# Two stored operands fewer, and the chopped-up sums of the fourth product on another timetable, in a soft-routing MoE kernel

## The chip, the cores and the metric

The kernel runs on one core of one Trainium2 chip. The metric is the device time of one execution in microseconds; the median of the runs counts, lower is better.

## The reference

Every token goes through all eight experts, and the results are added with the softmax of its router logits as weights:

```python
probs = softmax(router_logits)                       # 16 x 512 x 8
for e in range(8):
    output += probs[:, :, e:e+1] * (x @ expert_weights[e])
# x: 16 x 512 x 512, expert_weights: 8 x 512 x 2048, output: 16 x 512 x 2048, float32
```

## The kernel before

**One large product.** The sum over the experts is one matrix product `Z W`. `Z` has 8192 rows (tokens) and 4096 columns (the product of a probability and `x`, for each expert and each of 512 inputs). `W` holds the eight expert matrices one below the other. Operands are f16, sums f32.

**Seven products in place of eight, twice.** `Z` is cut into 16 row pairs `q`; each has a block `a = 2q` and a block `b = 2q + 1` of 256 rows. Its columns are cut into experts 0 to 3 and 4 to 7, and `W` into two halves of columns. A Strassen-like scheme makes the result of a row pair from seven products, P1 to P7, of sums of these quarters. Each is cut again in the same way into seven steps, in the order `STEPS = (1, 5, 6, 2, 7, 3, 4)`. A step is eight matmuls of 128x128 by 512 columns into one PSUM bank. The steps of the inner scheme use three banks of a product in turn: bank `x` for the steps 1, 6, 7 and 4, bank `q` for 5 and 3, bank `b` for 2. After a step, VectorE (DVE) or ScalarE (ACT) reads the bank (`post`), so a bank must have been read before the next step that uses it.

**Left operands** (class `Left`) are made on DVE from `x` (tile `xT`), probabilities that a DMA spreads over the partitions (`pT`) and a scratch tile `u`. For P5 it is `x_b` times the sums of the probabilities of both halves (`PQ`). P6 takes this one less `x_a` times `P1`. P7 takes `x_a P1 - x_b P1` (two products and a difference for each half). P3 wants `x_a P2` less the operand of P6, so every operand of P6 is stored in DRAM (`keep_z`, two transfers of 512 KB, tensor `z`) and fetched again as one of 1 MB (`ZBlock`).

**Right operands** are made from the weights by DVE and kept in 15 tiles `w` of 1 MB (pool `wpool`). Two products run side by side, which takes 14 of them. The sums for P7 and P4 don't fit beside them. `by_parts` makes them in the 15th tile, in four *quarters* each. A quarter goes through three hooks: `begin` loads four pieces (POOL's queue), `go_on` (P4 alone) subtracts `t2` from three of them and stores the differences as `t4` (`less_t2`), and `end` makes four sums in place (`sums_in_place`), each overwriting a piece and each stored at once (`wd<-w`, POOL's queue). Before the products begin, `turnover` fetches the 1 MB operands one by one through ACT's queue (`fetch_w`, line 164, `w<-wd`).

**Stages and slots.** `add` lists 56 stages, numbered from 0, of one or two products. In a stage with two, the steps alternate, 14 slots of 8 matmuls each. Stage 15 is `k5`: P5 of the pairs 0 and 1. Stage 16 is P6 of pair 0 alone. Stages 17 to 30 pair P6 of `q` with P5 of `q + 1`. Stage 31 (`k7`) is P6 of pair 15 and P7 of pair 0, stages 32 to 46 pair P4 of `q` with P7 of `q + 1`. Stage 47 (`k3`) is P4 of pair 15 and the first P3, stages 48 to 54 hold two P3 each, and stage 55 (`end`) the P3 of pair 15, which writes the result out itself. "21:8" below is slot 8 of stage 21. Counting matmuls along the trace puts the start of stage 17 at 437.0 us, of 21 at 533.7, of 22 at 557.9, of 23 at 584.1, of 28 at 710.8, of 31 at 784.0, of 32 at 811.2, of 46 at 1151.6, of 47 at 1175.8 and of 54 at 1340.2.

**Order.** The order of all instructions is written out by hand, and each engine works through its own in order. `at(stage, slot, make)` hooks a piece of work to a slot; `slots_after` counts slots on from a place. DVE's work goes into a `queue` of tasks with costs: `slack` lets out as many after each slot as a planned clock has room for, and `later(..., True)` puts a task ahead of the queue. `joined` (three tasks at the slots 12 and 13, a fourth at slot 3) is such: it takes P5's result from a tile of stored sums `h<-kept`, fetched by SP's queue. `start_loads` issues the loads of the stage after next after the first slot (`late` and `wait_for` change that slot, and the slot from which the left operands are queued).

Of the kernel before, what the change touches and what calls it, by code (L numbers as in the profile page):

```python
# [31 lines left out]
def kernel(  # L32
# [87 lines left out]
    def pool(o, i, **how):  # L120
        note(nc.gpsimd.dma_start(out=o, in_=i, **how))  # L121
# [12 lines left out]
    def new_w():  # L134
        return wpool.tile([P, K8, NB], f16, name="w", tag="w")
# [66 lines left out]
    P1, P2, PQ = 0, HE, 2 * HE  # L202
# [167 lines left out]
    def flush(task):  # L370
        while task is not None and not task.done:
            queue.popleft().run()

    def need(task):
        if task is not None and not task.done:
            flush(task)
            clock["pe"] = max(clock["pe"], clock["dve"])
# [244 lines left out]


    QK = 9
    ND = QK // 2

    def out_rows(q, odd, cols, tn):
        t, n = tn
        return out_f[ds((2 * q + odd) * HQ + t * HP, HP), ds(cols * NH + n * NB, NB)]

    def to_out(q, odd, cols, **how):
        return lambda tn, o: pool(out_rows(q, odd, cols, tn), o, **how)
# [18 lines left out]
    hooks, late, wait_for = {}, {}, {}  # L651

    def at(stage, slot, make):
        hooks.setdefault((stage, slot), []).append(make)

    def add(*products):
        stages.append(products)
        return len(stages) - 1
# [6 lines left out]
    def xblock(h):  # L665
        if h not in xs:
            xs[h] = XBlock(h)
        return xs[h]

    def left_of(r, q, fresh=True):  # L670
        a, b = 2 * q, 2 * q + 1
        if r == 1:
            pt = PBlock(a, P1, xp1[q - 2][1] if q in (2, 3) else None)
            if q in (2, 3):
                xs[a] = XBlock(a, xp1[q - 2][0])
            return Left(xblock(a), pt), [xblock(a), pt]
        if r in (2, 4):
            h, pt = (a, PBlock(a, P2)) if r == 2 else (b, PBlock(b, P2))
            return Left(xblock(h), pt), [xblock(h), pt]
        if r == 5:  # L680
            pt = PBlock(b, PQ)
            return Left(xblock(b), pt), [xblock(b), pt]
        if r == 6:
            pt = PBlock(a, P1)
            return Left(xblock(a), pt, of=lefts[5, q]), [xblock(a), pt]
        if r == 3:
            pt, kept_z = PBlock(a, P2), ZBlock(q)
            return Left(xblock(a), pt, kept=kept_z), [xblock(a), pt, kept_z]
        pa, pb = PBlock(a, P1), PBlock(b, P1)
        return Left(xblock(a), pa, (xblock(b), pb)), [xblock(a), pa, xblock(b), pb]  # L690

    def kept_rows(q):
        return lambda tn: kept[q][tn[1], ds(tn[0] * HP, HP), :]

    def product(r, q, **how):
        left, loads = left_of(r, q)
        lefts[r, q] = left
        p = None
        if r == 1:
            def sink(tn, o):  # L700
                pool(kept_rows(q)(tn), o)
            p = Product(right[1], left, sink)
        elif r == 2:
            if q >= QK:
                base = products[1, q].o.__getitem__
            else:
                base = bases[2, q] = Base(kept_rows(q))
            p = Product(right[2], left, to_out(q, 0, 0), base)
        elif r == 5:
            bases[6, q] = m1 = Base(kept_rows(q))  # L710
            m1.task = {}

            p = Product(right[5], left, to_out(q, 1, 0))
        elif r == 6:
            m1 = bases[6, q]

            def base(tn):
                need(m1.task[tn])
                return m1.t[tn]
            p = Product(right[6], left, to_out(q, 0, 1), base)  # L720
        elif r == 7:
            base = bases[7, q] = Base(lambda tn: out_rows(q, 0, 1, tn))
            p = Product(right[7], left, to_out(q, 1, 1), base)
        elif r == 4:
            p = Product(right[4], left, to_out(q, 1, 0, accum_op=ADD), products[7, q].o.__getitem__)
        else:
            p = Product(right[3], left, to_out(q, 0, 1, accum_op=ADD), **how)
        p.loads = loads
        products[r, q] = p
        return p  # L730
# [121 lines left out]

    for q in range(2, QK, 2):
        add(product(1, q), product(1, q + 1))
    for q in range(QK, 15):
        add(product(2, q), product(1, q + 1))
    forget(*range(0, 2 * QK, 2))
    rest = [15] + list(range(QK))
    for i in range(0, QK + 1, 2):
        k = add(product(2, rest[i]), product(2, rest[i + 1]))  # L860
# [5 lines left out]
    k5 = add(product(5, 0), product(5, 1))  # L866
# [3 lines left out]
    some = product(6, 15)  # L870
# [3 lines left out]
        add(product(4, q), product(7, q + 1))  # L874
    some = product(4, 15)
    xs.clear()
    k3 = add(some, product(3, 0))
    for q in range(1, 15, 2):
        add(product(3, q), product(3, q + 1))
    end = add(product(3, 15))  # L880
    late[k3 - 1] = 6
# [11 lines left out]
    for q in range(16):  # L893
        k = k5 + 1 + q
# [37 lines left out]
    def wedge_at(stage, slot, kn, e, then):  # L932
        made = []

        def begin():
            casts, made_ = wedge(kn, e)
            casts()
            made.extend(made_)

        def go_on():  # L940
            for make in made:
                later(1.22, make)
        at(stage, slot, begin)
        at(*then, go_on)

    b21, t1, t2, t3 = {}, {}, {}, {}
# [7 lines left out]
    def sums_at(stage, slot, r, of, ps):  # L954
        def go():
            if right[r].w is None:
                right[r].sums = right[r].build(of)
            for p in ps:
                right[r].queue_sum(right[r].sums, p)
        at(stage, slot, go)  # L960
    sums_at(ND - 1, 3, 2, b21, (5,))
    sums_at(ND - 1, 5, 2, b21, (6,))
    sums_at(ND - 1, 7, 2, b21, (7,))
    sums_at(ND - 1, 12, 2, b21, (4,))
    for i, (kn, e) in enumerate((kn, e) for kn in ((0, 0), (1, 0), (1, 1)) for e in range(2)):
        wedge_at(ND + i, 2, kn, e, (ND + i, 11))

# [60 lines left out]
    def slots_after(stage, slot, n):  # L1028
        slot += n
        while slot >= 7 * len(stages[stage]):  # L1030
            slot -= 7 * len(stages[stage])
            stage += 1
        return stage, slot
# [6 lines left out]
    def by_parts(stage, slot, every, r, load, between, when):  # L1040

        for j in range(4):
            b, chunks = {}, ds(2 * j, 2)

            def begin(b=b, j=j, chunks=chunks):
                flush(last_part[0])
                t = new_w()
                for i, kn in enumerate(ORDER):
                    b[kn] = t[:, ds(2 * i, 2), :]
                    load(b[kn], kn, j, chunks)  # L1050

            def go_on(b=b, chunks=chunks):
                for kn in b:
                    if kn != ODD:
                        between(b[kn], kn, chunks)

            def end(b=b, chunks=chunks):
                last_part[0] = sums_in_place(lambda p, o: pool(part_of((r, p), (0, 0), chunks), o), b, r, 0.69)
            at(*slots_after(stage, slot, j * every), begin)
            if between is not None:  # L1060
                at(*slots_after(stage, slot, j * every + when[0]), go_on)
            at(*slots_after(stage, slot, j * every + when[-1]), end)
# [8 lines left out]
    def load_part(what):  # L1071
        def load(t, kn, j, chunks):
            pool(t, part_of(what, kn, chunks))
        return load
# [10 lines left out]
    def keep_raw(t, kn, chunks):  # L1085
        pool(part_of("b22", kn, chunks), t)

    by_parts(k5 + 2, 4, 14, 7, load_part("t3"), None, (7,))
    by_parts(*slots_after(k5 + 2, 4, 60), 24, 4, load_p4, less_t2, (8, 15))
    by_parts(k7 + 4, 4, 36, 3, cast_part(22), keep_raw, (9, 16))  # L1090


# [16 lines left out]
    turnover(k7, 0, 4, "t4")  # L1109
    turnover(k3 - 1, 1, 3, "b22", 2)  # L1110

    for q in range(16):
        z_dram[q] = dram.tile([P, 2 * K8, HQ], f16, name=f"z_{q}")

        def keep_z(k, q=q):
            sp(z_dram[q][:, ds(k * K8, K8), :], lefts[6, q].t[k])
        k, half_way = k5 + 1 + q, 7 * len(stages[k5 + q]) * 9 // 14
        at(k - 1, half_way, lambda keep_z=keep_z: keep_z(0))
        at(k, 0, lambda keep_z=keep_z: keep_z(1))

    def load_z(q):
        load = products[3, q].loads[-1]
        load.by_hook = True
        return load.begin
    at(k3, 0, load_z(1))
    at(k3, 2, load_z(2))
    third3 = {}

    def third_of_p3(p):
# [2 lines left out]
        later(2.76, make)  # L1132
    at(k3, 3, lambda: third_of_p3(1))
    at(k3, 5, lambda: third_of_p3(5))
    wait_for[k3] = 7


    finish = products[3, 15]
# [33 lines left out]

    for stage in range(1, ND):
        thirds[stage] = Thirds(*(p.left for p in stages[stage]), third)
# [44 lines left out]
```

## Time and profile before

| | us |
|---|---|
| runs: median (lowest, highest) of 3 | 1383.44 (1380.64, 1385.46) |
| the profiled execution: its own time | 1381.43 |
| its span, first to last instruction | 1379.7 |
| TensorE matmul (PE) busy | 1362.8 (99%) |
| VectorE (DVE) busy | 1121.1 (81%) |
| GpSimd (POOL) busy | 411.6 (30%) |
| ScalarE (ACT) busy | 206.8 (15%) |

The profile is of one execution. Its span is 1.7 us shorter than the time of that execution, and that time is 2.0 us below the median of the runs. PE is TensorE's matmuls, PEld its weight loads, SPq and ACTq the queues through which SyncE and ScalarE issue DMAs. In rows of groups, `out<-in` names the tiles; behind the bar stand busy time, mean duration in ns, and the idle time of the engine just before, with what ended it. In rows of waits the three numbers are the sum, the count and the longest. In rows of windows each engine has its busy time and, in brackets, its instructions; then come the granted share of TensorE's clock, the share of the DMA engines and GB/s.

### The profile page before, as it was taken

Reading aid. Unit: us, or ns where it says so; the run is one execution under the profiler, and the core shown is the slowest. Engines: PE = TensorE matmul, PEld = TensorE weight load, DVE = VectorE, ACT = ScalarE, POOL = GpSimd, SP = SyncE. Lnnn points to the kernel's source line nnn. Section 1 sums busy time; section 2 is a strip of 40 time slices with the busy share of each in tenths; the row PEclk is TensorE's granted clock in tenths of the full one; section 3 lists DMA queues with packets and bytes.
Section 4 is the critical chain, followed back from the end, with each engine's and each line's share of the span. In section 5 each row is a group of like instructions: output and inputs, shape, how many; then the busy total and the mean of one; then the engine's idle time right before and its main releaser. Section 6 shows DMA issues by size and latency. Waiting matters only on the chain.

```text
span 1379.7 us, 18165 instructions
## 1 busy us (share of the span) xinstructions
PE 1362.8 (99%) x6630; PEld 645.9 (47%) x6630; DVE 1121.1 (81%) x1354; ACT 206.8 (15%) x397; POOL 411.6 (30%) x652
## 2 busy tenths in 40 slices
PE   9999999999999999989999989999999999999998
PEld 4555444444444444434444434444444444556554
DVE  7877767579789898588878878888889898898884
ACT  3232111100011111111111100000000000233331
POOL 3223233331222333243242112233342422223231
PEclk9999999999999999999999999999999999999999
DMA  9998999999799999999999998888897979999976
GB/s 184 217 266 219 214 258 248 260 292 391 235 293 294 302 330 297 296 269 310 306 268 327 376 398 267 178 241 209 228 265 209 257 207 281 343 298 231 235 107 126
DMA packets 193578, 363.23 MB, mean 263 GB/s; under 512 B 53200, under 2 KB 87248, under 8 KB 187728
## 3 DMA queue, kind: packets, MB, share of 16 engines
q0 software_dynamic: 88688, 185.12, 57.1%
q1 hardware_dynamic: 100768, 148.51, 35.2%
q10 hardware_dynamic: 4032, 28.44, 5.3%
q8 instruction: 52, 0.85, 0.2%
q14 instruction: 38, 0.31, 0.1%
HBM read 216.04 MB, written 173.21 MB: 282 GB/s over the span
## 4 chain that ended last, share of the span: by engine, by line
PE 64%; issue 15%; DMA 14%; POOL 6%; DVE 1%; POOLq 0%; ACT 0%; SPq 0%; DVEq 0%; ACTq 0%
PE ps L130 48%; PE pt L130 16%; DMA wd<-w 5%; POOL out_dram L121 3%; DMA w<-in_expert_weights_dram 3%; DMA out_dram<-h 3%; DMA w<-wd 2%; POOL w L121 1%; DMA z<-z 1%; POOL wd L121 1%; POOL xs L121 0%; DVE z L107 0%; DVE h L107 0%; POOLq L121 0%; DVE w L107 0%
## 5 line engine op out<-in xcount | busy, mean ns | idle before, releaser
L130 PE MATMUL ps<-w,z 128*128 128x512 f16 (+1 forms) x3704 | 812.5, 376 | 6.4 <-DMA w<-wd 3.6
L130 PEld LDWEIGHTS <-z 128*128 128x128 f16 x5336 | 521.8, 98 | 613.8 <-issue 6.1
L121 POOL DMA_DIRECT2D out_dram<-h x380 | 248.9, 680 | 701.7 <-ACT h L614 342.3
L130 PE MATMUL pt<-w,z 128*128 128x512 f16 (+1 forms) x1632 | 357.8, 369 | 2.0 <-DVE h L107 1.5
L107 DVE TENSOR_TENSOR h<-ps,h 128x512 f32<-128x512 f32 x260 | 177.0, 687 | 115.2 <-PE ps L130 101.4
L107 DVE TENSOR_TENSOR z<-xT,pT 128x2048 f16<-128x2048 f16 x220 | 266.6, 1217 | 2.6 <-issue 1.9
L130 PE MATMUL ps<-w,d 128*128 128x512 f16 x880 | 200.8, 382 | 2.9 <-DVE ps L107 2.9
L107 DVE TENSOR_TENSOR h<-pt,h 128x512 f32<-128x512 f32 x155 | 105.6, 687 | 52.2 <-PE pt L130 46.3
L130 PEld LDWEIGHTS <-d 128*128 128x128 f16 x880 | 86.5, 98 | 106.2 <-issue 5.6
L107 DVE TENSOR_TENSOR z<-z,d 128x2048 f16<-128x2048 f16 x110 | 132.5, 1216 | 0.0
L107 DVE TENSOR_TENSOR w<-w 128x1024 f16<-128x1024 f16 (+2 forms) x108 | 111.5, 1041 | 22.6 <-DMA wd<-w 12.9
L614 ACT COPY h<-ps 128x512 f32<-128x512 f32 x64 | 37.4, 586 | 491.7 <-PE ps L130 426.0
L601 ACT COPY h<-ps 128x512 f32<-128x512 f32 x90 | 52.7, 586 | 374.9 <-PE ps L130 343.9
L107 DVE TENSOR_TENSOR d<-z 128x1024 f16<-128x1024 f16 x110 | 74.7, 684 | 0.9
L107 DVE TENSOR_TENSOR ps<-ps,h 128x512 f32<-128x512 f32 (+1 forms) x86 | 54.0, 629 | 20.8 <-PE ps L130 16.5
L121 POOL DMA_DIRECT2D wd<-w x86 | 48.3, 584 | 58.0 <-DVE w L107 43.3
L121 POOL DMA_DIRECT2D w<-in_expert_weights_dram x65 | 48.9, 785 | 44.8 <-DMA wd<-w 34.9
L107 DVE TENSOR_TENSOR h<-h 128x512 f32<-128x512 f32 (+2 forms) x69 | 45.2, 676 | 9.5 <-DMA h<-kept 9.4
L121 POOL DMA_DIRECT2D kept<-h x56 | 30.8, 550 | 70.1 <-ACT h L601 38.4
L597 ACT COPY h<-ps 128x512 f32<-128x512 f32 x65 | 36.4, 601 | 79.7 <-PE ps L130 72.8
L593 ACT COPY ps<-ps 128x512 f32<-128x512 f32 x45 | 25.6, 570 | 115.0 <-PE ps L130 77.8
L107 DVE TENSOR_TENSOR z<-z,w 128x2048 f16<-128x2048 f16 x32 | 39.2, 1225 | 1.7 <-DMA w<-z 0.7
(72 smaller groups left out, 371.8 us busy)
## 6 DMA issues: line engine op xcount, KB each, us to landing
out_dram<-h POOLq DMA_DIRECT2D x380, 256.0 KB, 7.2
pT<-p_dram SPq DMA_DIRECT2D x124, 256.0 KB, 7.8
w<-wd ACTq DMA_DIRECT2D x27, 1024.0 KB, 9.4
h<-kept SPq DMA_DIRECT2D x100, 256.0 KB, 8.1
wd<-w POOLq DMA_DIRECT2D x72, 256.0 KB, 6.4
xT<-x SPq DMA_DIRECT2D x71, 256.0 KB, 9.0
w<-in_expert_weights_dram POOLq DMA_DIRECT2D x35, 512.0 KB, 9.9
h<-out_dram SPq DMA_DIRECT2D x68, 256.0 KB, 5.4
```

Of the source, the lines that this page charges most:

```text
L107: dve(nc.vector.tensor_tensor(out=o, in0=a, in1=b, op=op))
L121: note(nc.gpsimd.dma_start(out=o, in_=i, **how))
L130: note(nc.tensor.matmul(ps, z, w, start=start, stop=stop, skip_group_check=True))
L593: act(nc.scalar.copy(self.banks["b"], x))
L597: act(nc.scalar.copy(o[tn], q if p == 5 else x))
L601: act(nc.scalar.copy(o[TN[p]], b if p == 2 else x))
L614: act(nc.scalar.copy(o[tn], b))
```

## The change

P3's operand is made anew for the row pairs 14 and 15, in the way P7's is made (`x_a PQ - x_b PQ`), so that P6's operands of these two pairs aren't stored or fetched. The P3 in stage 47 is that of pair 14 in place of pair 0, and the stages 48 to 54 take the pairs 0 to 13. The fetches of the stored operands of the pairs 0 and 1 are hooked to 46:10 and 47:2 (before: pair 0 among the loads of its stage, 1 and 2 at 47:0 and 47:2). The second store of each operand of P6 goes from slot 0 of its stage to slot 5. The quarters for P7 begin 13 slots apart (before 14). Those for P4 begin 56 slots after the first of P7's (before 60), 28 apart (before 24), with `go_on` 9 and `end` 20 slots behind the begin (before 8 and 15). The left operands behind stage 47 are queued from slot 6 (before 7).

```diff
+    KEPT_Z = 14
...
-        if r == 3:
+        if r == 3 and q < KEPT_Z:
             pt, kept_z = PBlock(a, P2), ZBlock(q)
             return Left(xblock(a), pt, kept=kept_z), [xblock(a), pt, kept_z]
-        pa, pb = PBlock(a, P1), PBlock(b, P1)
+        pa, pb = PBlock(a, P1 if r == 7 else PQ), PBlock(b, P1 if r == 7 else PQ)
         return Left(xblock(a), pa, (xblock(b), pb)), [xblock(a), pa, xblock(b), pb]
...
-    k3 = add(some, product(3, 0))
-    for q in range(1, 15, 2):
+    k3 = add(some, product(3, KEPT_Z))
+    for q in range(0, KEPT_Z, 2):
         add(product(3, q), product(3, q + 1))
     end = add(product(3, 15))
...
-    by_parts(k5 + 2, 4, 14, 7, load_part("t3"), None, (7,))
-    by_parts(*slots_after(k5 + 2, 4, 60), 24, 4, load_p4, less_t2, (8, 15))
+    by_parts(k5 + 2, 4, 13, 7, load_part("t3"), None, (7,))
+    by_parts(*slots_after(k5 + 2, 4, 56), 28, 4, load_p4, less_t2, (9, 20))
     by_parts(k7 + 4, 4, 36, 3, cast_part(22), keep_raw, (9, 16))
...
-    for q in range(16):
+    for q in range(KEPT_Z):
         z_dram[q] = dram.tile([P, 2 * K8, HQ], f16, name=f"z_{q}")
...
         at(k - 1, half_way, lambda keep_z=keep_z: keep_z(0))
-        at(k, 0, lambda keep_z=keep_z: keep_z(1))
+        at(k, 5, lambda keep_z=keep_z: keep_z(1))
...
-    at(k3, 0, load_z(1))
-    at(k3, 2, load_z(2))
+    at(k3 - 1, 10, load_z(0))
+    at(k3, 2, load_z(1))
...
-    wait_for[k3] = 7
+    wait_for[k3] = 6
```

| quarter | begin, go_on, end before | begin, go_on, end after |
|---|---|---|
| P7, 1 | 17:4, -, 17:11 | 17:4, -, 17:11 |
| P7, 2 | 18:4, -, 18:11 | 18:3, -, 18:10 |
| P7, 3 | 19:4, -, 19:11 | 19:2, -, 19:9 |
| P7, 4 | 20:4, -, 20:11 | 20:1, -, 20:8 |
| P4, 1 | 21:8, 22:2, 22:9 | 21:4, 21:13, 22:10 |
| P4, 2 | 23:4, 23:12, 24:5 | 23:4, 23:13, 24:10 |
| P4, 3 | 25:0, 25:8, 26:1 | 25:4, 25:13, 26:10 |
| P4, 4 | 26:10, 27:4, 27:11 | 27:4, 27:13, 28:10 |

## The prediction

> **What bounds the kernel now.** I read the page's totals first, then the windows of 20 us through the span, then the timeline where a window falls short, then the chain of waits.
>
> ```profile
> span 1379.7 us, 18165 instructions
> PE 1362.8 (99%) x6630; PEld 645.9 (47%) x6630; DVE 1121.1 (81%) x1354; ACT 206.8 (15%) x397; POOL 411.6 (30%) x652
> ```
>
> PE is busy for 99%, and the change leaves all 6630 matmuls in place. It can only win back what PE stands still. The windows show where (PE busy and, in brackets, its matmuls; the clock share stands behind POOL):
>
> ```profile
> 560.00:580.00 20.00, 18.11 (x85) 8.13 (x84) 16.66 (x21) 2.91 (x5) 4.20 (x9) 1.00 1.14 308
> 580.00:600.00 20.00, 16.18 (x67) 6.86 (x66) 12.82 (x18) 1.74 (x3) 5.52 (x10) 0.91 1.04 328
> 600.00:620.00 20.00, 20.00 (x94) 9.08 (x93) 16.69 (x22) 2.91 (x5) 9.45 (x16) 1.00 1.06 219
> 700.00:720.00 20.00, 19.45 (x91) 8.76 (x90) 12.41 (x19) 2.33 (x4) 9.49 (x17) 1.00 1.06 294
> 800.00:820.00 20.00, 17.10 (x80) 7.63 (x79) 15.51 (x19) 1.07 (x2) 4.32 (x8) 1.00 1.02 412
> 820.00:840.00 20.00, 18.39 (x86) 8.08 (x84) 16.47 (x21) 1.17 (x2) 5.74 (x8) 1.00 1.02 357
> ...
> 840.98 3.45 PE pt L130 x16
> ```
>
> A full window holds 94 matmuls, and 16 in a row take 3.45 us in the chain, so 0.2156 us each and 1.73 us a slot. The five short windows lack 9, 27, 3, 14 and 8, together 61 x 0.2156 = 13.2 us. Between the head and the tail of the span no other window lacks any. So the three places are 560 to 600 (stages 22 and 23, 7.8 us), 700 to 720 (stage 28, 0.6 us) and 800 to 840 (the turnover in stages 31 and 32, 4.7 us), and 13.2 us is the most that the change can bring.
>
> **Stages 22 and 23.** The timeline there:
>
> ```profile
> 564.77 3.62 PE L130 MATMUL ps<-w,d 128*128 128x512 f16 x16
> ...
> 569.39 0.69 DVE L107 TENSOR_TENSOR h<-h 128x512 f32<-128x512 f32 x1 [2.90 <-DMA h<-kept]
> ...
> 573.73 3.61 PE L130 MATMUL ps<-w,z 128*128 128x512 f16 x16 [1.89 <-DVE h L107]
> ...
> 576.59 1.28 DVE L107 TENSOR_TENSOR w<-w 128x1024 f16<-128x1024 f16 x2
> ...
> 577.57 1.14 POOL L121 DMA_DIRECT2D wd<-w  x2 [4.28 <-DVE w L107]
> ...
> 587.11 1.42 DVE L107 TENSOR_TENSOR w<-w 128x1024 f16<-128x1024 f16 x2 [7.44 <-DMA wd<-w]
> ...
> 589.18 3.61 PE L130 MATMUL pt<-w,z 128*128 128x512 f16 x16 [1.49 <-DVE h L107]
> ...
> 595.13 5.30 PE L130 MATMUL ps<-w,d 128*128 128x512 f16 x16 [2.33 <-DVE ps L107]
> ```
>
> The first quarter for P4 stores its differences from 577.57 on and then overwrites one of them. DVE stands 7.44 us until that store has left the tile, about 9.5 us after its issue. Everything that DVE does for PE is queued behind: PE stops for 1.49 and 2.33 us, and the 16 matmuls behind take 5.30 in place of 3.62 us, 1.68 more, in the slice whose clock share is 0.91. That makes 5.5 of the 7.8 us. In code the hooks are 7 slots, 12.1 us, apart. On DVE they are not: `less_t2` is hooked to 22:2 (561.3 us) but queued behind the operands of stage 23, and runs at 576.59, right ahead of the sums.
>
> The change hooks it to 21:13, ahead of the point where the operands are queued (after 22:0), so it should run at about 556 to 561. The sums stand at 22:10, 575.1 us: 14 us apart or more, against the 9.5 that the store took. I take the wait as gone, with some 4 us to spare. Stage 28 lost its 0.6 us in the same way, in the fourth quarter (27:4 and 27:11 before):
>
> ```profile
> DVE w L107 <- DMA wd<-w: 5.5, 1, 5.5
> ```
>
> All four quarters get the same phase, slot 13 and slot 10 of the next stage, so this goes too.
>
> [...]
>
> The other part, the stop of 1.89 us, comes from a fetch `h<-kept` that landed late. It can be followed back through two queues:
>
> ```profile
> 540.70 1.07 POOL L121 DMA_DIRECT2D wd<-w  x2 [1.79 <-DMA out_dram<-h]
> 541.77 0.73 POOL L121 DMA_DIRECT2D xs<-in_x_dram  x1
> ...
> 552.91 2.87 SPq L415 DMA_TRANSPOSE xT<-xs  x2
> ...
> 559.01 9.23 SPq L118 DMA_DIRECT2D pT<-p_dram  x2
> 568.34 0.85 SPq L118 DMA_DIRECT2D h<-kept  x2
> ```
>
> The load of `x` stands on POOL behind the last two sums of P7's fourth quarter, so the transposes on SP start at 552.91, and the second `pT` and both `h<-kept` wait behind them until 568. That quarter's end moves from 20:11 to 20:8, 5.2 us earlier, and the second store of `z` leaves the place ahead of these loads for slot 5. That brings the chain forward by up to 5.2 us, more than the 2.90 that DVE waited. I take 0.8 us as left over, since the landings stay long. So 7.8 - 0.8 = 7.0 us here, 0.6 in stage 28. Bounds for both: 0 (the wait only moves) and 8.4.
>
> **The turnover.** The chain in order of time, DMA issues by line, a window and ACT's timeline:
>
> ```profile
> 784.79 14.33 DMA z<-z
> ...
> 799.20 10.27 DMA w<-wd
> ...
> 821.65 12.20 DMA w<-wd
> ```
> ```profile
> h<-out_dram SPq DMA_DIRECT2D x9, 256.0 KB, 12.3
> ```
> ```profile
> 784.00:811.00 27.00, 24.10 (x112) 10.79 (x111) 21.15 (x26) 1.66 (x3) 4.32 (x8) 1.00 1.01 399
> ```
> ```profile
> 784.41 0.33 SPq L118 DMA_DIRECT2D h<-out_dram  x1
> ```
> ```profile
> 790.16 0.58 ACT L601 COPY h<-ps 128x512 f32<-128x512 f32 x1 [15.73 <-DVE h L107]
> ```
>
> PE waits for P7's last operand. Its fetch was issued at 799.20, when the last store of P6's operand (pair 15, issued at 784.79) had landed. The two share no tile. In the program SP's and ACT's transfers take eight semaphores in turn, so an issue waits for the eighth before it. The change removes this store and the three ahead of it, 2 MB in all. The eighth before the fetch is then the `h<-out_dram` issued at 784.41. By the median of 12.3 us it lands at 796.7, so the fetch goes 2.5 us earlier. It can't go before 790.2, where ACT's copy held the queue. The DMA engines are full here (share 1.01), so without 1 MB at 399 GB/s, 2.6 us, things land no later. The next fetch, P4's last, landed at 821.65 + 12.20 = 833.85, again late. PE arrives earlier now and may only wait longer there. So the gain lies between 0 and 4.7 us, and I take 2.4, what the nearer wait gives.
>
> **What it adds.**
>
> ```profile
> L107 DVE TENSOR_TENSOR z<-xT,pT 128x2048 f16<-128x2048 f16 x220 | 266.6, 1217 | 2.6 <-issue 1.9
> L107 DVE TENSOR_TENSOR z<-z,w 128x2048 f16<-128x2048 f16 x32 | 39.2, 1225 | 1.7 <-DMA w<-z 0.7
> ...
> 1160.00:1180.00 20.00, 20.00 (x94) 9.09 (x93) 14.14 (x17) 1.68 (x3) 5.67 (x8) 1.00 1.00 324
> 1340.00:1360.00 20.00, 20.00 (x122) 11.79 (x121) 11.53 (x15) 7.64 (x17) 5.06 (x7) 1.00 0.77 142
> ```
>
> Four multiplications more, 4 x 1.22 = 4.9 us of DVE; the subtractions stay. Two run in stage 46, two in 54. DVE has 5.9 and 8.5 us free in the windows there, so I put them at nothing; without that cover each pair costs at most 2.4. Their four loads of 256 KB for each pair replace a fetch of 1 MB and a load or two, as many as every stage from 31 to 46 issues for P7 without a short window. Fetching the stored operands of pairs 0 and 1 at 46:10 and 47:2 lengthens no queue: before, the second of a pair also came at 47:2, and DVE waited 0.7 us for `z` in the whole run. Queued a slot earlier, DVE could wait 1.7 us more. A bank is read three slots, 5.2 us, before it is needed again, and that hides it. The store of `z` at slot 5 is moved on SP past one `xT`, two `pT`, two `h<-kept` and a store of `x`, all of which gain; its tile is held 8.6 us longer, to about slot 5 + 14.33 us = 23 us of a stage of 24.2, where PE uses it up to slot 12. Nothing, at most 1.
>
> P7's quarters come 13 slots apart, and this is the part with a price:
>
> ```profile
> 499.68 2.14 POOL L121 DMA_DIRECT2D w<-wd  x4 [8.55 <-DMA wd<-w]
> ...
> 525.12 2.14 POOL L121 DMA_DIRECT2D w<-wd  x4 [11.42 <-DMA wd<-w]
> ```
> ```profile
> 485.78 1.41 DVE L107 TENSOR_TENSOR w<-w 128x1024 f16<-128x1024 f16 x2
> ...
> 530.25 0.69 DVE L107 TENSOR_TENSOR w<-w 128x1024 f16<-128x1024 f16 x1 [0.86 <-DMA w<-wd]
> ```
>
> POOL already stands 8.55 and 11.42 us at a begin until the last quarter's stores have landed, and DVE waits for the load. With the sums a slot earlier each time DVE may wait 1.7, 3.5 and 5.2 us if the stores land no sooner. But of the sums hooked to 18:11, at 480.2 us, two ran only at 485.78, behind the `joined` tasks of the slots 12 and 13. From the slots 10, 9 and 8 they run ahead of these, and I estimate that the stores end 3 to 4 us earlier. I expect waits of 1 to 2 us, under the 5.2 that a bank's turn hides, so nothing; at most 1.7 us of PE for the fourth.
>
> **Sum.** 7.0 + 0.6 + 2.4 = 10.0 us. The profiled execution took 1381.4, so its like would take 1371.4. The median of the runs lies 2.0 above it, so the forecast is 1373.4. A difference of 0.3%, 4.15 us, is about what a measurement of this kernel can tell from none.
>
> **Rivals.**
>
> Only the overwriting wait goes. Then 5.5 + 0.6 = 6.1, 1377.3. The late `h<-kept` stays because DMA, not the queues, is late (share 1.14 in its window), and PE waits at 833.85 for what it doesn't wait for earlier. For it: both landings are over 10 us. Against: 2 MB less, and a queue freed 5.2 us sooner. Chance 0.2.
>
> The distance exists in slots only. If DVE's queue is late at 21:13 as well and `less_t2` still runs close to the sums, the change doesn't do what it says. Only the turnover's 2.4 are left: 1381.0, no change that can be told. Against it: operands for stage 22 are queued a full stage before 21:13. Chance 0.1.
>
> Slower: P4's loads come late for their differences, in all four quarters alike.
>
> ```profile
> 552.34 10.41 DMA w<-in_expert_weights_dram
> ...
> 600.62 0.73 POOL L121 DMA_DIRECT2D w<-in_expert_weights_dram  x1 [4.05 <-DMA wd<-w]
> ```
>
> From slot 4 to 13 are 15.5 us, and a load took 10.41. POOL may thus be held 5.1 us before DVE waits, and 10.3 before PE does. The end of one quarter and the begin of the next are now 8 slots apart, 13.8 us. If each quarter cost what the first did, 4 x 5.5 = 22.0, less 8.5 for what goes all the same: 1396.9. It decides from three quarters on. For it: holds of 11.42 exist. Against: at the second quarter, with 9 slots, POOL stood 4.05. Chance 0.12.
>
> **Numbers.** The forecast's own case has 0.58. Faster is it and the first rival, 0.78; same 0.10; slower 0.12. With all 13.2 us gone the median would be 1370.2, and the runs scatter by some 2 us, so the range begins at 1369. It ends at 1381.5, behind the second rival, and leaves out the third.
>
> **What would show it.** In the changed profile no DVE wait `w <- DMA wd<-w` over 2 us, windows in the stages 22, 23 and 28 with 94 matmuls and clock 1.00, no `z<-z` in the chain near 790, and some PE wait for `w<-wd` left in stage 31 or 32. DVE waits for `w<-wd` of over 5 us in the stages 18 to 20, for `w<-in_expert_weights_dram` in 21 to 28, or short windows near 1180 or 1340 would prove me wrong.

## The result and the profile after

The changed kernel takes 1368.92 us (median of 6 runs, 1368.38 to 1369.49). The kernel before, run beside it, took 1382.04 (6 runs, 1376.03 to 1385.46). The ratio is 0.9912, with an interval of 0.9887 to 0.9937, so it is faster, by 13.1 us by the medians and 12.2 by the ratio; 10.0 were forecast, and the median lies 0.08 us under the low end of the range. (Three more runs beside it brought the median of before from 1383.44 to 1382.04.) The runs also lie closer together: 1.1 us from lowest to highest, against 9.4.

The page of the profile after (this execution took 1368.82 us):

```profile
span 1367.0 us, 18181 instructions
PE 1359.6 (99%) x6630; PEld 645.4 (47%) x6630; DVE 1124.8 (82%) x1358; ACT 207.3 (15%) x397; POOL 411.8 (30%) x652
```

The span is 12.7 us shorter with the same 6630 matmuls, so it is time in which PE stood still or ran slowly before. The windows of the changed kernel (PE busy and its matmuls first, the clock share behind POOL) at the places that were short, and at the ends where two P3 operands are now made anew:

```profile
560.00:580.00 20.00, 20.00 (x95) 9.02 (x93) 18.46 (x24) 2.91 (x5) 6.31 (x12) 1.00 0.95 286
580.00:600.00 20.00, 20.00 (x94) 9.07 (x93) 16.70 (x21) 3.50 (x6) 6.98 (x12) 1.00 1.08 293
700.00:720.00 20.00, 20.00 (x94) 9.08 (x93) 18.29 (x23) 3.50 (x6) 5.55 (x10) 1.00 0.94 319
800.00:820.00 20.00, 19.68 (x92) 8.80 (x90) 17.62 (x20) 1.17 (x2) 2.00 (x3) 1.00 1.03 393
820.00:840.00 20.00, 19.51 (x91) 8.74 (x90) 17.27 (x22) 1.17 (x2) 5.46 (x8) 1.00 0.84 257
...
1160.00:1180.00 20.00, 20.00 (x94) 9.07 (x93) 16.00 (x21) 2.91 (x5) 3.79 (x6) 1.00 1.04 369
...
1340.00:1360.00 20.00, 20.00 (x95) 9.04 (x93) 8.70 (x12) 1.76 (x3) 6.87 (x8) 1.00 0.80 106
```

The stages 22, 23 and 28 are full, the turnover lacks about five matmuls, and the late windows are full too. The timeline of the first P4 quarter (DVE, with POOL's stores between):

```profile
558.02 1.28 DVE L107 TENSOR_TENSOR w<-w 128x1024 f16<-128x1024 f16 x2
...
559.34 1.07 POOL L121 DMA_DIRECT2D wd<-w  x2
...
575.87 1.41 DVE L107 TENSOR_TENSOR w<-w 128x1024 f16<-128x1024 f16 x2
```

The differences run 17.9 us ahead of the sums, and the sums carry no wait (before: 10.5 us ahead, and a wait of 7.44). P7's quarters on POOL, and behind them the load of `x` that stood at 541.77 before:

```profile
484.20 0.54 POOL L121 DMA_DIRECT2D wd<-w  x1 [0.66 <-DVE w L107]
...
494.05 2.15 POOL L121 DMA_DIRECT2D w<-wd  x4 [5.22 <-DMA wd<-w]
...
515.26 2.14 POOL L121 DMA_DIRECT2D w<-wd  x4 [3.46 <-DMA wd<-w]
...
535.32 0.72 POOL L121 DMA_DIRECT2D xs<-in_x_dram  x1
```

The begins of the third and fourth quarters are held 5.22 and 3.46 us where it was 8.55 and 11.42, and the load of `x` goes out 6.4 us sooner. At the turnover, the issues of the four fetches, in ACT's queue, end at 785.22 where they ended at 800.00. Before, and then after:

```profile
790.18 9.82 ACTq L164 DMA_DIRECT2D w<-wd  x4
```
```profile
783.00 2.22 ACTq L164 DMA_DIRECT2D w<-wd  x4
```

Of PE's waits for fetches one is left there, for the next of them (another 0.3 us are a wait for DVE):

```profile
PE ps L130 <- DMA w<-wd: 0.5, 1, 0.5
```

### The profile page after: what moved, and what is told of

Its sections match the earlier page's. It is cut to its first block, busy times and chain, and to the rows that moved or that the text cites. A ratio compares the mean times of both kernels' runs of the same rounds, so it can differ in the third digit from the quotient of the medians.

```text
span 1367.0 us, 18181 instructions
## 1 busy us (share of the span) xinstructions
PE 1359.6 (99%) x6630; PEld 645.4 (47%) x6630; DVE 1124.8 (82%) x1358; ACT 207.3 (15%) x397; POOL 411.8 (30%) x652
## 4 chain that ended last, share of the span: by engine, by line
PE 97%; DMA 3%; POOL 0%; issue 0%; ACT 0%; DVE 0%; ACTq 0%; POOLq 0%; DVEq 0%
PE ps L130 71%; PE pt L130 25%; DMA h<-out_dram 2%; DMA w<-wd 1%; DMA w<-in_expert_weights_dram 1%; POOL w L121 0%; ACT h L614 0%; DVE ps L107 0%; ACT h L1168 0%; ACTq L164 0%; POOL ident L225 0%; POOLq L225 0%; DVEq L107 0%; POOLq L1204 0%
## 5 line engine op out<-in xcount | busy, mean ns | idle before, releaser
L107 DVE TENSOR_TENSOR z<-z,u 128x2048 f16<-128x2048 f16 x36 | 44.1, 1225 | 1.2
L107 DVE TENSOR_TENSOR u<-xT,pT 128x2048 f16<-128x2048 f16 x36 | 43.8, 1216 | 0.0
## 6 DMA issues: line engine op xcount, KB each, us to landing
w<-in_expert_weights_dram POOLq DMA_DIRECT2D x35, 512.0 KB, 10.5
```

The source lines that it names most:

```text
L107: dve(nc.vector.tensor_tensor(out=o, in0=a, in1=b, op=op))
```

## How the experiments are read

The loss of a kernel is counted in two windows: 440 to 770 us (stages 17 to 30) and 770 to 850 (the turnover). At 0.2156 us for a matmul the first holds 1531 and the second 371 if PE never stops or slows down; each that lacks is 0.2156 us. The rows of before and of after:

```profile
440.00:770.00 330.00, 323.75 (x1491) 146.05 (x1490) 271.25 (x338) 46.62 (x80) 107.07 (x191) 0.99 1.06 300
770.00:850.00 80.00, 75.49 (x349) 33.87 (x348) 65.93 (x79) 4.94 (x9) 14.38 (x24) 1.00 0.97 362
```
```profile
440.00:770.00 330.00, 330.00 (x1531) 149.61 (x1529) 279.00 (x347) 48.37 (x83) 108.72 (x194) 1.00 1.04 310
770.00:850.00 80.00, 79.19 (x367) 35.61 (x365) 67.18 (x82) 4.10 (x7) 17.89 (x28) 1.00 0.98 338
```

Before lacks 40 and 22 (8.6 and 4.7 us), after 0 and 4 (0 and 0.9). All kernels in one table; the losses are of the one profiled execution, the ratio is to the kernel before on the same chip:

| kernel | median (lowest to highest, runs) | ratio | lost 440-770, 770-850 |
|---|---|---|---|
| after | 1368.92 (1368.38-1369.49, 6) | 0.9912 [0.9887, 0.9937] | 0, 0.9 |
| e1: P4's table as before | 1373.98 (1367.56-1377.94, 7) | 0.9934 [0.9906, 0.9961] | 4.7, 1.5 |
| e2: P4's table alone | 1383.50 (1378.27-1386.47, 10) | 1.0008 [0.9987, 1.0029] | 5.8, 7.3 |
| e3: differences two slots later | 1371.13 (1368.43-1377.83, 6) | 0.9921 [0.9895, 0.9947] | 8.6, 0.9 |
| e4: all of `z` kept | 1375.11 (1372.94-1378.80, 8) | 0.9952 [0.9937, 0.9968] | 0, 7.8 |
| e5: P7's quarters 14 apart | 1375.17 (1368.17-1380.35, 9) | 0.9939 [0.9916, 0.9962] | 0.4, 1.3 |
| e6: second store at slot 0 | 1368.85 (1368.11-1369.34, 4) | 0.9908 [0.9888, 0.9927] | 0, 0 |
| e7: slot 5 alone | 1383.65 (1375.14-1388.28, 10) | 1.0016 [0.9994, 1.0037] | 0, 6.9 |
| e8: `z` stored on POOL's queue, not read | 1370.74 (1370.32-1371.35, 4) | 0.9922 [0.9903, 0.9941] | 0, 2.8 |
| e9: `z` part alone | 1374.41 (1371.56-1378.34, 10) | 0.9952 [0.9934, 0.9970] | 4.1, 2.6 |
| e10: P7's quarters 13 apart alone | 1375.73 (1372.73-1383.74, 10) | 0.9959 [0.9936, 0.9983] | 0, 7.5 |
| e11: sums five slots sooner | 1368.91 (1368.04-1369.53, 5) | 0.9909 [0.9882, 0.9937] | 0, 0.6 |

The profiled execution is one draw: that of e3 is its highest run (1377.83), that of e7 its lowest (1375.14), that of e5 one of its low ones (1369.62). Where a kernel's runs scatter, the runs together say what a part is worth, and the profile only by which wait. For runs in two groups the median is itself a rough measure: it stands in the larger group. So differences of medians between two changed kernels are given with the differences of their ratios, times 1381 us, behind them.

## The experiments: P4's table

**e1**: the change without P4's table.

```diff
-    by_parts(*slots_after(k5 + 2, 4, 56), 28, 4, load_p4, less_t2, (9, 20))
+    by_parts(*slots_after(k5 + 2, 4, 60), 24, 4, load_p4, less_t2, (8, 15))
```

> The changed kernel with P4's quarters alone back on the old timetable (60, 24, (8, 15)). Theory A (the differences were queued behind the operands of the next stage and so ran right ahead of the sums): DVE waits 5 to 8 us for wd<-w in the first quarter and 4 to 6 in the fourth, PE loses 5 to 6 us around stages 22 and 23 and up to 1 in stage 28: 1374 to 1377. Rival B (P7's earlier quarters, or the store of z in slot 5, were what freed the queues): no wait over 2 us, 1369 to 1370.

The median is 5.1 us above that of after (3.0 by the ratios), but three of the seven runs (1367.56 to 1367.98) take no longer than the changed kernel, and the other four lie between 1373.98 and 1377.94. So P4's new table takes away something that happens in some executions and not in others. The profiled run is one of the four. In it the overwriting waits of DVE are back, but the longest is 1.6 us where 5 to 8 were forecast, and a late `h<-kept` stands above them in DVE's list:

```profile
DVE h L107 <- DMA h<-kept: 4.4, 1, 4.4
...
DVE w L107 <- DMA wd<-w: 3.2, 2, 1.6
```

PE's one long stop, 2.08 us, comes behind those 4.4. The trace leads back to POOL: the begin of P4's third quarter stood 7.13 us there, until 639.08, for the second quarter's stores; the load of `x` behind it went out at 641.77 and landed 11.2 us later, the transposes followed at 652.97 and `h<-kept` at 656.48. So in this execution the old table costs PE its time through POOL's queue, and not by the overwriting.

**e2**: P4's table put into the kernel before, and nothing else (e1's diff the other way round).

> The kernel before with P4's new timetable alone. Theory A: no wait of DVE for wd<-w over 2 us, the 5.5 + 0.6 us in stages 22, 23 and 28 are gone, the 1.9 us of the late h<-kept may stay, the turnover's 4.7 us stay: 1375 to 1378 against 1382. Rival B: the waits stay, since P7's fourth quarter still ends at 20:11 and holds POOL until after 550 us: 1380 or more.

Nothing is won. In its list of DVE's waits the wait on `wd<-w` for the tile `w` is gone, and another stands first:

```profile
DVE h L107 <- DMA h<-kept: 18.9, 7, 5.0
```

Before, its row reads 9.4 us in 6. PE now stops for that one, as its list in the same window shows:

```profile
PE ps L130 <- DVE h L107: 4.3, 3, 1.7
```

In this profile the stages 17 to 30 still lose 5.8 us (8.6 before), and the turnover loses 7.3 in place of 4.7. The forecast of 1375 to 1378 missed.

**e3**: the differences at 22:1 in place of 21:13, still 9 slots ahead of the sums (before: 7).

```diff
-... load_p4, less_t2, (9, 20))
+... load_p4, less_t2, (11, 20))
```

> The changed kernel with go_on of P4's quarters 11 slots behind the begin in place of 9, so in the slot after the operands of the next stage are queued; the sums stay at 20. 9 slots, 15.5 us, remain between the two hooks, against 7 before and 11 in the changed kernel. Theory A: DVE runs the differences only some 8 slots later, right ahead of the sums, and waits 5 to 8 us for the store in each of four quarters; PE loses about 5 us in each: 1383 to 1391. Rival C (the distance in slots is what counts): 15.5 us are more than the 9.5 of a store, so at most 1 us: 1369 to 1370.

The median is 2.2 us above after's (1.2 by the ratios), which neither forecast has: 1383 to 1391 was far off, and four of the six runs take 1371.43 us or less. But in the profiled run, the slowest, the wait is back, though the distance in slots is wider than before. DVE's list of waits and its timeline at the first quarter in e3:

```profile
DVE w L107 <- DMA wd<-w: 15.9, 3, 8.4
```

```profile
571.86 1.29 DVE L107 TENSOR_TENSOR w<-w 128x1024 f16<-128x1024 f16 x2
...
579.69 1.42 DVE L107 TENSOR_TENSOR w<-w 128x1024 f16<-128x1024 f16 x2 [3.46 <-DMA wd<-w]
```

The wait does not always reach PE: behind the first and the third quarter PE does not stop, behind the second and the fourth it stops for up to 2.56 and 2.33 us.

**e11**: the differences stay at 21:13, and the sums come five slots sooner, so that only 6 slots lie between, fewer than before.

```diff
-... load_p4, less_t2, (9, 20))
+... load_p4, less_t2, (9, 15))
```

> The changed kernel with P4's sums 15 slots behind the begin in place of 20: 6 slots behind the differences, fewer than the 7 of before, but the differences stay ahead of the operands of the next stage in DVE's queue and the sums behind them. Theory A (the place in the queue): no overwriting wait over 3 us, 1369 to 1371. Rival C (the distance in slots): overwriting waits of 5 us and more in each quarter, 1372 to 1385.

No wait, and the time of the changed kernel. DVE's timeline in e11:

```profile
558.35 1.29 DVE L107 TENSOR_TENSOR w<-w 128x1024 f16<-128x1024 f16 x2
...
576.19 1.41 DVE L107 TENSOR_TENSOR w<-w 128x1024 f16<-128x1024 f16 x2
```

The sums are hooked to 22:5, some 566 us, and run 10 us later, behind the operands of stage 23. What counts is that the differences are ahead of these operands in DVE's queue and the sums behind; e3 has both behind, with 9 slots between the hooks and 7.8 us between the two on DVE (after: 17.9). For this wait the wider spacing of the sums in the change is not what helps; the earlier `go_on` is. The other two numbers of the table, 56 and 28, no run tests alone.

## The experiments: P7's quarters and slot 5

**e5**: the change with P7's quarters 14 apart again (the first of P4's stays at 21:4).

```diff
-    by_parts(k5 + 2, 4, 13, 7, load_part("t3"), None, (7,))
+    by_parts(k5 + 2, 4, 14, 7, load_part("t3"), None, (7,))
```

> The changed kernel with P7's quarters 14 slots apart again (the first of P4's then begins at 21:4 all the same). The run with P4's timetable alone showed the late fetches h<-kept as the wait that takes over (18.9 us of DVE). Theory P (they are late because POOL's loads of x stand behind P7's sums): h<-kept waits of over 5 us come back, 2 to 6 us of PE in the stages 21 to 30: 1371 to 1375. Theory S (they are late because of the place of the store of z on SP): nothing comes back, 1369 to 1370.

The median is 6.3 us above after's (3.7 by the ratios), again with two groups: three runs of 1368.17 to 1369.62 and six of 1373.49 to 1380.35. The profiled run is one of the three, and PE loses 0.4 us in its stages 17 to 30; but the wait for `h<-kept` is back on DVE:

```profile
DVE h L107 <- DMA h<-kept: 10.2, 3, 4.4
```

**e10**: 13 apart in the kernel before, and nothing else (this diff the other way round).

> The kernel before with nothing but P7's quarters 13 slots apart (the first of P4's keeps its place, 21:8). In the runs so far POOL stood 33 to 36 us for a begin between 440 and 790 us where P7's quarters were 13 apart, 49 to 56 where they were 14, and DVE waited for h<-kept in all of the latter. Theory P: POOL's waits at the begins fall to 33 to 42 us, h<-kept waits to under 5; overwriting waits stay, and the turnover's loss: 1376 to 1380. Rival Q (the 13 helps only together with P4's timetable): POOL over 45 us, 1381 to 1383.

It wins 0.41% (0.17 to 0.64), some 5.7 us, with one number changed. POOL's wait for the tile `w`, stages 17 to 30, in before and in e10:

```profile
POOL w L121 <- DMA wd<-w: 51.7, 7, 12.9
```
```profile
POOL w L121 <- DMA wd<-w: 40.3, 6, 11.7
```

In the changed kernel it is 33.2, in e2, which wins nothing, 56.2. Over all profiles it is 43.4 to 56.2 in the five kernels with 14 slots and 28.9 to 40.3 in the eight with 13; DVE's wait for `h<-kept` is 4.1 to 18.9 us in the five and 0 to 4.4 in the eight, whatever else they change. And in DVE's list in e10 the late fetch is all but gone, although nothing was done to P4's table; DVE still waits 6.0 us for `wd<-w`, and PE feels none of it in these stages:

```profile
DVE w L107 <- DMA wd<-w: 6.0, 3, 4.0
...
DVE h L107 <- DMA h<-kept: 0.7, 1, 0.7
```

The two windows of e10, the first full, the second lacking 35:

```profile
440.00:770.00 330.00, 330.00 (x1531) 149.61 (x1529) 279.52 (x346) 48.38 (x83) 108.79 (x194) 1.00 1.04 310
770.00:850.00 80.00, 74.50 (x336) 33.02 (x334) 63.85 (x78) 4.00 (x7) 14.17 (x23) 0.98 0.94 340
```

Its longest stop there, 2.00 us and 8 matmuls in 3.21 us behind it (1.89 in its other rows; the granted clock is 0.92 from 805 to 826 us), goes back to a store of `z`. Each of these three was issued when the one above it had landed, though they share no tile, and DVE's work for PE waited for the last:

```profile
771.18 14.71 DMA z<-z
...
785.96 13.12 DMA xT<-x
...
799.16 15.49 DMA h<-out_dram
```

**e6**: the change with the second store of `z` at slot 0 again. **e7**: slot 5 put alone into the kernel before.

```diff
-        at(k, 5, lambda keep_z=keep_z: keep_z(1))
+        at(k, 0, lambda keep_z=keep_z: keep_z(1))
```

> The changed kernel with the second store of P6's operand back in slot 0. Theory S (ahead of the loads of the stage, its landing of 10 to 14 us is waited for by the transposes, the eighth transfer behind it, and h<-kept waits for these): h<-kept waits of over 5 us come back, 2 to 8 us of PE in the stages 17 to 30: 1371 to 1377. Theory P (POOL's timetable is what counts): 1369 to 1370.

> The kernel before with nothing but the second store of P6's operand in slot 5. Theory S: the waits for h<-kept (9.4 us of DVE before) fall under 2; the overwriting waits of DVE (12.9) stay; PE wins 2 to 4 us of the 8.4 in the stages 22, 23 and 28: 1378 to 1380 against 1382. Theory P: 1381 to 1383.

Neither direction moves the time: 0.9908 against 0.9912, and 1.0016 with an interval that holds 1. Slot 5 is worth nothing that these runs can tell. (The profile of e7 has full stages 17 to 30, but it is of that kernel's fastest run.)

## The experiments: the operands that are not kept

**e4**: the change, but all sixteen operands of P6 stored and fetched as before.

```diff
-    KEPT_Z = 14
...
-        if r == 3 and q < KEPT_Z:
+        if r == 3:
...
-    for q in range(KEPT_Z):
+    for q in range(16):
...
-    at(k3 - 1, 10, load_z(0))
-    at(k3, 2, load_z(1))
+    at(k3, 0, load_z(1))
+    at(k3, 2, load_z(2))
...
-    wait_for[k3] = 6
+    wait_for[k3] = 7
```

> The changed kernel with all of P6's operands kept again and P3 in the old order (pairs 0; 1, 2; ...); the timetables and the store in slot 5 stay. Theory A (the last stores of z held up P7's last operand by the turn of the semaphores): a PE wait for w<-wd of 2 to 3 us in stage 31, turnover 3 to 5 us short of matmuls: 1372 to 1374. Rival D (the turnover was late only because of what had gone wrong before it): 1369 to 1370.

The stages 17 to 30 stay full, and the turnover loses 7.8 us, more than before the change and more than the 3 to 5 forecast:

```profile
770.00:850.00 80.00, 74.81 (x335) 33.10 (x334) 63.64 (x77) 4.10 (x7) 14.18 (x23) 0.96 0.96 339
```

SP's and ACT's queues in e4, then PE:

```profile
772.95 0.49 SPq L118 DMA_DIRECT2D z<-z  x1
...
787.60 2.31 ACTq L164 DMA_DIRECT2D w<-wd  x4
...
803.67 7.89 PE L130 MATMUL ps<-w,z 128*128 128x512 f16 x24 [5.19 <-DMA w<-wd]
```

The fetches go out 4.6 us later than after the change; the first of them waits until a store of `z` of pair 15 has landed. The third, the one for which PE waits, goes out at 789.03, when an `h<-out_dram` issued at 777.29 has landed. PE, which now comes to the turnover without having lost anything, stops for 5.19 us, and the 24 matmuls behind take 7.89 us in place of 5.35 (the time of 24 in e2's row in the last section), with a granted clock of 0.83 from 790 to 810 us. That makes 7.7 of the 7.8. In e7, which also keeps `z` and whose profiled run comes to the turnover in time, the same wait is 5.19 us too.

**e9**: the `z` part put alone into the kernel before (e4's diff the other way round, on before).

> The kernel before with nothing but P6's operands of the pairs 14 and 15 made anew in P3 (order of P3, fetches at 46:10 and 47:2, operands queued from slot 6 included), all timetables and the store's slot as before. Theory A: the turnover loses under 2 us of the 4.7, the stages 22, 23 and 28 lose what they lost, 5 to 9 us: 1375 to 1379. Rival U (what is won at the turnover depends on PE coming on time from the stages before): 1380 to 1383.

It wins 0.48% (0.30 to 0.66), 6.6 us, which rules out the rival; the turnover loses 2.6 us where under 2 were forecast. Its profiled run:

```profile
440.00:770.00 330.00, 326.44 (x1512) 147.80 (x1511) 274.37 (x342) 48.35 (x83) 107.75 (x192) 1.00 1.05 304
770.00:850.00 80.00, 77.74 (x359) 34.77 (x358) 68.89 (x82) 4.14 (x8) 15.68 (x26) 1.00 0.96 341
```

The first row lacks 19 against 40, most of it in stages where this kernel issues the same instructions as the one before: the first store that it leaves out would come in stage 29, behind 735 us. So over 4 us between two profiles in the stages 17 to 28 can be scatter, and only the step from 4.7 to 2.6 us in the second row may be put down to the edit.

**e8**: the change, with the operands of the pairs 14 and 15 stored all the same, from POOL's queue, and never read. Their 2 MB are moved, but their semaphores are not those that SP and ACT take in turn (in the trace of before the 554 transfers of these two carry eight semaphores, those of POOL eight others; the store of `z` at 784.79 and the fetch at 799.20 carry the same).

```diff
-    for q in range(KEPT_Z):
+    for q in range(16):
...
-            sp(z_dram[q][:, ds(k * K8, K8), :], lefts[6, q].t[k])
+            (pool if q >= KEPT_Z else sp)(z_dram[q][:, ds(k * K8, K8), :], lefts[6, q].t[k])
```

> The changed kernel, but P6's operands of the pairs 14 and 15 are stored all the same, by POOL's queue in place of SP's, and never read. The bytes are there, the places in SP's and ACT's turn of eight semaphores aren't. Theory A (the turn): P7's last operand is issued in time, no PE wait for w<-wd over 1 us in stage 31: 1368 to 1370. Rival T (the 2 MB in a full stretch of DMA): the operands land 2 to 5 us later, PE waits in the stages 31 and 32: 1371 to 1375.

1370.74 against 1368.85 of e6 on the same chip, which differs otherwise only in slot 5: the bytes (and four issues on POOL) cost 1.9 us, between the two forecasts. ACT's queue in e8 issues the fetches nearly as early as after the change,

```profile
784.28 2.00 ACTq L164 DMA_DIRECT2D w<-wd  x4
```

and PE waits 2.0 us for `w<-wd` in the whole turnover, 1.55 of it in stage 31. With the stores on SP's queue (e4) the fetches start at 787.60 and the median is 1375.11. So of the 6 us that the `z` part is worth (6.2 by the medians, 5.5 by the ratios), some 2 are bytes and some 4 go with the later issue. That the later issue comes from the eight semaphores in turn fits all of e4, e8 and the changed kernel, but e4 also makes the P3 operands in the old way, so it isn't the only difference between the two.

## Why the prediction was right, and where it was not

**What bounds it**: right. PE's stops in the three places were 13.2 us; 0.9 are left, and the span is 12.7 shorter. Elsewhere between head and tail one window, 1200 to 1220, lacks 0.1. All the signs named for it came, and none of those against it.

**The overwriting wait, 5.5 + 0.6 us**: the wait went as worked out (17.9 us between differences and sums against a forecast of 14 or more), and the reason, the place in DVE's queue, is shown by e3 and e11. The step that failed is putting these 6.1 us down to it. Without the other parts, removing it wins nothing (e2), because the late `h<-kept` comes next, which was said to be a stop of 1.9 us of its own, and the turnover loses more. On top of the other parts P4's table is worth 5.1 us by the medians (3.0 by the ratios), in some executions only, and in the one that e1's profile shows the loss came through POOL's queue and `h<-kept`. How much of it is the overwriting wait is not shown. The wait that a trace shows last is not the worth of its cause when a second one stands close behind.

**P7's quarters, costed at nothing and called the part with a price**: the price was right, the gain was missed. Only the fourth quarter's end was counted, as a part of the 1.5 us that the sum leaves for `h<-kept` (7.0 less 5.5). The last store of the second quarter goes out at 484.20 (before, by the trace, at 488.84), so the estimate of 3 to 4 us was near, with 4.6; DVE's wait for `w<-wd`, forecast at 1 to 2 us, is one of 1.7. What was not carried on is that with POOL free sooner the whole chain of `x`, transposes and `h<-kept` comes sooner in every stage: 5.7 us alone (e10), 6.3 when taken out of the change (e5; 3.7 by the ratios). That a hold of 51.7 us on a queue could be shortened was in the profile.

**The timetables together, 7.6 us**: e4 has them without the `z` part (slot 5, worth nothing, included) and wins 0.48% (0.32 to 0.63), 6.6 us. Right in size, in part by luck: by e4's profile all 8.6 us of the stages 17 to 30 came back and 3.1 more went at the turnover. Wrong in the split.

**The turnover, 2.4 us**: this term was mis-sized. The fetch for which PE waited, the third of the four, goes out 15.2 us sooner (784.00 for 799.20). 8.6 us of that only say that PE itself comes sooner, since nothing is lost ahead; the other 6.6 stand against a forecast of 2.5. The mechanism was right: the fetch follows the landing of the `h<-out_dram` that the prediction named, issued at 775.24 and landed at 783.9. But that landing took 8.7 us where the median of 12.3 was put in (the trace of before has 13.4 for this transfer, 784.41 to 797.81). 3.8 us of the 4.7 went. And the term was measured from a kernel that came late to the turnover: with the stages before it full, a kernel that keeps `z` loses 7.8, 6.9 and 7.5 us there (e4, e7, e10). Alone the `z` part is worth 6.6 us (e9), in the change 6.2 by the medians (e4; 5.5 by the ratios).

**Slot 5 and DVE's extra work, nothing**: right. DVE is busy 3.7 us more, and no late window is short.

**The rivals**: the first had the right mechanism, PE arriving earlier and only waiting longer, and it is what e4, e7 and e10 show; removing the stores prevents it. The second named what decides (e3), but at 21:13 the queue was not late. The slower one did not come: no DVE wait for `w<-in_expert_weights_dram` is left between 440 and 850, and a begin of P4 on POOL was held 5.26 us at the second quarter, just above the bound of 5.1:

```profile
591.20 0.73 POOL L121 DMA_DIRECT2D w<-in_expert_weights_dram  x1 [5.26 <-DMA wd<-w]
```

**The sum**: 10.0 us were forecast between two profiled executions, and they lie 12.6 apart (1381.43 and 1368.82). 1.4 of the difference is the turnover, 0.8 what was taken as left over in the stages 22 and 23, and 0.4 isn't placed. The forecast lies 4.5 us above the median; the other 1.9 are the 2.0 us by which the runs of before stood above their profile, which those of after don't (0.1). The scatter went with its cause, the way I read it: the queues have a margin now, so a single late landing no longer reaches PE.

**Open**: taking out one part at a time (P4's table, P7's quarters, `z`, slot 5) costs 5.1, 6.3, 6.2 and 0 us by the medians, 17.6 together, where the whole is 13.1; by the ratios it is 3.0, 3.7, 5.5 and -0.6, together 11.6, where the whole is 12.2. Each of these has an interval of some 3 us or more, so whether the parts cover for each other isn't shown, apart from P4's table, which alone wins nothing that can be told. What sorts the runs of e1 and e5 into two groups isn't known, nor why e9 gains 6.6 us where its turnover row shows 2.1.

## What to carry to other kernels

Two waits close behind each other can't be added up from one trace: ask of each what ends next if it alone goes, and look for the queue that feeds both (here POOL's held begins). Distance between a store and its overwriting is a matter of the engine's own order, so find the bulk of work between the two hooks, not the number of slots (here 9 slots were 7.8 us in e3, and 6 slots 17.8 us in e11). When an early stage is sped up, re-cost the next fixed point in the order, here the fetches of the turnover, from the new arrival time.

## What the runs showed of the hardware

Behind short stops PE's clock sometimes dropped and sometimes did not. In e1 a stop of 2.08 us was followed by 16 matmuls in 5.30 us (3.62 in the rows on either side), in e2 one of 2.78 us by 24 in 5.35 us (5.34 in the trace of before at 821.60, with no stop ahead), with a granted clock of 1.00 from 800 to 820 us:

```profile
671.25 5.30 PE L130 MATMUL ps<-w,z 128*128 128x512 f16 x16 [2.08 <-DVE h L107]
```
```profile
809.05 5.35 PE L130 MATMUL ps<-w,z 128*128 128x512 f16 x24 [2.78 <-DMA w<-wd]
```

The kernel before has both in one execution: 16 matmuls in 5.30 us behind a stop of 2.33 (granted clock 0.91 from 580 to 600 us), and 24 in 5.36 us behind one of 2.90 (1.00 from 800 to 820 us).

The window of e1 around its stop has a granted clock of 0.86:

```profile
664.00:676.00 12.00, 9.92 (x39) 4.09 (x38) 8.98 (x11) 1.76 (x3) 1.82 (x4) 0.86 1.10 327
```

So a stop of 2 to 3 us was followed by a further loss of 1.68 us (5.30 for 3.62) in e1 and once in before, and by none in e2; what decides between the two no run shows. In the changed kernel the prediction's 1.68 us went together with the stops ahead of them (granted clock 1.00 from 560 to 600 us).
